# The last 256 output features of a two-layer trunk computed token-major in two halves of the tokens, each half finished and written on its own

## The chip, the cores and the metric

The kernel runs on one core of a Trainium2 chip. The metric is the device time of one execution in microseconds, as the median of several runs. A difference of 0.3% is 6.5 us here.

## The reference

Two pre-norm residual layers act on 256 tokens of 2048 features, all in float32. Each layer is a mixer followed by an MLP, and the output is a last RMSNorm of the residual stream. Only the end of the second layer and that norm matter here:

```python
def rms_norm(x, g):
    xf = x.astype(jnp.float32)
    y = xf * lax.rsqrt(jnp.mean(xf * xf, axis=-1, keepdims=True) + NORM_EPS)
    return (y * g.astype(jnp.float32)).astype(x.dtype)

def squared_relu_mlp(h, w_up, w_down):
    return jnp.square(jax.nn.relu(h @ w_up)) @ w_down
...
        h = rms_norm(x, mlp_norm[layer])
        x = x + squared_relu_mlp(h, w_up[layer], w_down[layer]).astype(x.dtype)
    return rms_norm(x, final_norm)
```

The last norm needs, for each token, the sum of squares over all 2048 features. So no feature of a token can be written before its last feature is known.

## The kernel before

The residual stream is kept feature-major in eight tiles `xT[0]` to `xT[7]`, each of 128 partitions x 2 x 256 tokens, so that a tile holds 256 features of all 256 tokens. Every weight chunk of 128 x 1024 floats is split into a rounded part `hi` (ScalarE, line 1336) and the rest `lo` (VectorE, line 1347). The activations are split the same way, and a product takes hi x hi, hi x lo and lo x hi, which are summed in PSUM. The work is written out in one list, `stream`, of pairs of a block and the number of one of its chunks. Line 1445 walks over it. A small scheduler, `jobs`, counts ticks, one per chunk here, and starts side jobs when they are due. On each engine, instructions run in the order in which the program issues them.

In the last MLP the hidden features are in eight groups. Six of them go through products that are summed in DRAM (`sums`), and come back token-major as `hs["sum", cb]`. The last two groups are multiplied at the end: eight blocks of 256 output features, `b` = 0 to 7, each with four chunks of four 128-row pieces of the weights (`eights`, line 1177). Blocks 0 to 6 are of kind "T": the weights are the stationary side and the 256 tokens (hi and lo side by side, 512 columns) the moving one. Ahead of a block's last chunk `add_sums` (line 1147) adds the transposed `hs["sum"]` to `xT[b]`. When a block ends, `down_done` (line 1162) adds the result to `xT[b]` and `final_block` (line 1228) starts a job, due two ticks later. The job adds the squares to `acc` (line 246 to 247), transposes the tile to token-major (line 1243) and stores it, times the gain, into the output tile `o` of 128 x 2 x 2048 (line 1245).

Block 7 is of kind "last". It has two PSUM regions in one tile, `ps[0]` and `ps[1]`, one in each of two PSUM banks, for its two groups of 128 features. Its last chunk does all of `ps[0]` ahead of all of `ps[1]` (line 449). Then `last_block` (line 1249) scales by `rB`, adds to `xT[7]`, squares, sums over partitions by matmuls with a column of ones (line 1262), transposes (line 1266), raises the mean to the power -0.5 on GpSimd (line 1278) and scales the whole output tile in four column quarters. VectorE takes the first 128 tokens (line 1284) and ScalarE the others (line 1285). SyncE issues eight writes of 256 KB (line 1287).

Functions that stay but are called by the change: `temp` and `side` give rotating buffers, three in SBUF and two in PSUM, and `banks(name, 1)` gives a PSUM tile of two banks.

Of the kernel before, what the change touches and what calls it, by code (L numbers as in the profile page):

```python
# [10 lines left out]
F32 = mybir.dt.float32  # L11
F32R = mybir.dt.float32r
BF16 = mybir.dt.bfloat16
AF = mybir.ActivationFunctionType
OP = mybir.AluOpType
X = mybir.AxisListType.X

P = 128
T = 256
D = 2048  # L20
KT = D // P
FF = 8192
EPS = 1e-6
# [22 lines left out]
class Jobs:  # L46
# [21 lines left out]
    def need(self, key):  # L68
        rounds = 0
        while key not in self.done:  # L70
            last = self.owner[key]
            for job in list(self.jobs):
                if job in self.jobs and not job[3]:
                    self.step(job)
                if key in self.done or job is last and rounds < 8:
                    break
            rounds += 1
# [49 lines left out]
class Block:  # L127


    def __init__(self, kind, chunks, mov, done, tiles=2, take=None, extra=None):  # L130
        self.extra = extra
        self.kind, self.chunks, self.mov, self.done, self.tiles = kind, chunks, mov, done, tiles
        self.total = len(chunks) if kind == "S" else sum(len(c.kts) for c in chunks)
        self.take = take
        self.count, self.ps = 0, None


# [1 line left out]
def trunk(ctx, tc, x, attn_norm, mlp_norm, w_up, w_down, ev_w_in, ev_q_norm, ev_w_uq, ev_kv_norm,  # L139
          ev_w_ukv, ev_w_out, od_w_in, od_sinks, od_w_out, final_norm, c_perm, c_rope, c_dist, out):  # L140
    nc = tc.nc
# [6 lines left out]
    jobs = Jobs(2)  # L148
# [10 lines left out]
    def side():  # L159
        return psum.tile([P, 512], F32, name="side", bufs=2)  # L160

    def temp():
        return tmp.tile([P, 2, T], F32, name="t", bufs=3)
# [36 lines left out]
    def banks(name="mm", bufs=3):  # L200

        return st["banks"].tile([P, 2, 512], F32, name=name, bufs=bufs)
# [232 lines left out]
    def add(block):  # L435
        for i in range(len(block.chunks)):
            stream.append((block, i))

    def consume(block, i, hi, lo):
        if block.kind == "S":  # L440
            return consume_products(block, i, hi, lo)
        if block.ps is None:
            block.ps = (block.take or banks)()
        ps, tiles, kts = block.ps, block.tiles, block.chunks[i].kts
        hi = hi[:, 0:len(kts) * tiles * P].rearrange("p (k c) -> p k c", c=tiles * P)
        lo = lo[:, 0:len(kts) * tiles * P].rearrange("p (k c) -> p k c", c=tiles * P)
        if block.kind == "N":
            order = [(n, tok) for n in range(len(kts)) for tok in range(2)]
        elif block.kind == "last" and block.count + len(kts) == block.total:
            order = [(n, j) for j in range(tiles) for n in range(len(kts))]  # L450
        else:
            order = [(n, j) for n in range(len(kts)) for j in range(tiles)]
        if block.extra and block.count + len(kts) == block.total:
            block.extra(ps)
        for n, j in order:
            m = block.mov(kts[n])
            first, last = block.count + n == 0, block.count + n == block.total - 1
            if block.kind == "N":
                o = ps[:, j, 0:T]
                xh, xl = m[:, j * P:(j + 1) * P], m[:, T + j * P:T + (j + 1) * P]  # L460
                mm(o, xh, hi[:, n], start=first, stop=False)  # L461
                mm(o, xh, lo[:, n], start=False, stop=False)  # L462
                mm(o, xl, hi[:, n], start=False, stop=last)  # L463
                continue
            c = slice(j * P, (j + 1) * P)
            if block.kind == "last":
                mm(ps[j], hi[:, n, c], m[:, 0:T], start=first, stop=False)
                mm(ps[j], hi[:, n, c], m[:, T:], start=False, stop=False)
                mm(ps[j], lo[:, n, c], m[:, 0:T], start=False, stop=last)
            else:  # L470
                if not last:
                    mm(ps[:, j], hi[:, n, c], m, start=first, stop=False)  # L472
                mm(ps[:, j, 0:T], lo[:, n, c], m[:, 0:T], start=False, stop=False)  # L473
                if last:
                    mm(ps[:, j], hi[:, n, c], m, start=False, stop=True)  # L475
        block.count += len(kts)
        if block.count == block.total:
            block.done(ps)

    def consume_products(block, i, hi, lo):  # L480

# [481 lines left out]
    def mlp(layer, last):  # L963
# [29 lines left out]
        def take_free(b):  # L993
            return lambda: banks(f"s{b % 2}", 1)

        def take_last():
            ps = banks("s1", 1)
            return [ps[:, j, 0:T] for j in range(2)]

        def up_done(grp, b):  # L1000
            def f(ps):
                t = temp()
# [144 lines left out]
        def add_sums(b):  # L1147

            def f(ps):
                need(("sum", b // 2))  # L1150
                need(("rB", n0))
                g, turned, t = hs["sum", b // 2], side(), temp()
                for j in range(2):
                    for tok in range(2):
                        nc.tensor.transpose(turned[:, j * T + tok * P:j * T + (tok + 1) * P],
                                            g[:, tok, b % 2, j * P:(j + 1) * P], ident)
                rB = E.setdefault("rB", st["rB"])
                tt(t, turned.rearrange("p (j t) -> p j t", t=T), rB[:, None, :].to_broadcast([P, 2, T]), op=OP.mult)
                tt(xT[b], xT[b], t, op=OP.add)
            return f  # L1160
# [58 lines left out]
        for b in range(8):  # L1219
            w = eights(wd, b * T, (NGRP - NS) * W // P)  # L1220
            if last and b == 7:
                add(Block("last", w, h_mov, lambda ps: last_block(E, ps), take=take_last, extra=add_sums(b)))
            else:
                add(Block("T", w, h_mov, down_done(b), take=take_free(b), extra=add_sums(b)))
        return open_pool, pool_ctx.close
# [2 lines left out]
    def final_block(E, b):  # L1228
        if b == 0:
            new_phase()  # L1230
            st["o"] = res.tile([P, 2, D], F32, name="xs")

        def job():
            yield 2, 1
            squares(b)
            if b == 6:
                acc = st["acc"]
                tt(acc[:, 0], acc[:, 0], acc[:, 1], op=OP.add)
            ps = side()
            pv = ps.rearrange("p (t c) -> p t c", c=T)  # L1240
            for tok in range(2):
                for j in range(2):
                    nc.tensor.transpose(pv[:, tok, j * P:(j + 1) * P], xT[b][:, j, tok * P:(tok + 1) * P], ident)
            fn = E["fn"](b * T, T)
            tt(st["o"][:, :, b * T:(b + 1) * T], pv, fn[:, None, :].to_broadcast([P, 2, T]), op=OP.mult)
        jobs.spawn(job())
        jobs.step(jobs.jobs[-1])

    def last_block(E, ps):

        jobs.drain()
        o, acc, xl = st["o"], st["acc"], xT[7]
        t, sq = temp(), temp()
        for j in range(2):
            tt(t[:, j], ps[j], E["rB"], op=OP.mult)
            tt(xl[:, j], xl[:, j], t[:, j], op=OP.add)
            act(sq[:, j], xl[:, j], AF.Square)
        sums, turn = banks("up", 1), side()

        def add_up(a, first, last):  # L1260
            for tok in range(2):
                mm(sums[:, tok, 0:1], a[:, tok * P:(tok + 1) * P], ones[:, 0:1], start=first, stop=last)

        def turn_out(j):
            for tok in range(2):
                nc.tensor.transpose(turn[:, j * T + tok * P:j * T + (tok + 1) * P], xl[:, j, tok * P:(tok + 1) * P], ident)
            c0 = 7 * T + j * P
            tt(o[:, :, c0:c0 + P], turn[:, j * T:(j + 1) * T].rearrange("p (t c) -> p t c", c=P),
               E["fn"](c0, P)[:, None].to_broadcast([P, 2, P]), op=OP.mult)

        add_up(acc[:, 0], True, False)
        turn_out(0)
        add_up(sq[:, 0], False, False)
        add_up(sq[:, 1], False, True)
        ms = tmp.tile([P, 2], F32, name="ms", bufs=2)
        nc.vector.tensor_scalar(ms, sums[:, :, 0], 1.0 / D, EPS, op0=OP.mult, op1=OP.add)
        r = res.tile([P, 2], F32, name="r", bufs=2)
        nc.gpsimd.tensor_tensor(r, ms, mhalf, op=OP.pow)
        turn_out(1)
        ov = out.rearrange("b (t p) d -> p (b t) d", p=P)  # L1280
        W = D // 4
        for q in range(4):
            c = slice(q * W, (q + 1) * W)
            nc.vector.tensor_scalar(o[:, 0, c], o[:, 0, c], r[:, 0:1], None, op0=OP.mult)
            act(o[:, 1, c], o[:, 1, c], AF.Copy, scale=r[:, 1:2])
            for tok in range(2):
                nc.sync.dma_start(ov[:, tok, c], o[:, tok, c])


    phases = []  # L1290
# [212 lines left out]
```

## Time and profile before

| what | us |
|---|---|
| median of 3 runs | 2158.56 (2158.47 to 2163.91) |
| the profiled execution's own time | 2162.11 |
| its span, first to last instruction | 2160.3 |
| last matmul of block 7 starts | 2147.44 |
| first write of the output is issued | 2152.16 |

Times in the rows are microseconds from the start of the span. PE is TensorE, PEld its weight load, DVE VectorE, ACT ScalarE, POOL GpSimd, SP SyncE; a q behind a name is the engine's instruction queue. "L1262" is line 1262 of the kernel.

### The profile page before, as it was taken

What the parts mean: (1) busy time and instruction counts of PE and PEld (TensorE: products, weight loads), DVE (VectorE), ACT (ScalarE), POOL (GpSimd) and SP (SyncE); (2) the same over time, 40 slices, a digit from 0 to 9 for tenths busy, and PEclk for the clock granted to TensorE, in tenths of its full rate; (3) what the DMA queues carried; (4) which work ended last, traced back from release to release, by engine and by line L of the source; (5) the groups of instructions that cost most, each with busy time, mean ns of one, the idle gap of its engine ahead of it and who ended that gap; (6) DMA issues with size and microseconds to landing.
All of it is one profiled execution on the core that took longest, in us unless ns stands there. A gap on an engine that the chain in (4) does not pass through costs nothing.

```text
span 2160.3 us, 35009 instructions
## 1 busy us (share of the span) xinstructions
PE 2141.6 (99%) x14038; PEld 1949.6 (90%) x14038; DVE 1588.6 (74%) x2120; ACT 1290.0 (60%) x1777; POOL 163.1 (8%) x217
## 2 busy tenths in 40 slices
PE   9999999999999999999999999999999999999998
PEld 7898988999999999988888889989999999999887
DVE  6766666788888888857766665577888888887475
ACT  6554545676666666655545436456676767676542
POOL 0000000000000000331000000000000000013310
PEclk9999999999999999999999999999999999999999
DMA  8545446668988989997554455666788889899972
GB/s 259 179 145 163 157 167 208 204 222 247 251 239 241 249 240 258 248 283 218 174 171 142 156 176 165 161 201 195 232 245 248 241 243 244 245 252 249 291 213 87
DMA packets 313812, 459.43 MB, mean 213 GB/s; under 512 B 11865, under 2 KB 198305, under 8 KB 313649
## 3 DMA queue, kind: packets, MB, share of 16 engines
q1 hardware_dynamic: 288416, 392.32, 57.5%
q0 software_dynamic: 25200, 64.86, 15.7%
q8 instruction: 110, 1.80, 0.3%
q14 instruction: 54, 0.43, 0.1%
q10 hardware_dynamic: 32, 0.01, 0.0%
HBM read 404.73 MB, written 60.82 MB: 215 GB/s over the span
## 4 chain that ended last, share of the span: by engine, by line
PE 49%; issue 39%; DMA 8%; POOL 4%; ACT 0%; POOLq 0%; SPq 0%; DVE 0%; ACTq 0%
PE mm L472 15%; PE mm L473 8%; PE s L472 6%; DMA sums<-sums 6%; PE s L473 4%; POOL sums L1127 3%; PE mm L461 2%; PE mm L463 2%; PE mm L462 2%; PE up L472 1%; DMA sums<-stage 1%; PE mm L475 1%; PE side L352 1%; PE up L473 1%; PE s L495 1%
## 5 line engine op out<-in xcount | busy, mean ns | idle before, releaser
L1347 DVE TENSOR_TENSOR lo<-raw,hi 128x1024 fp32r<-128x1024 f32 (+2 forms) x804 | 853.7, 1082 | 210.9 <-PE mm L473 74.8
L1336 ACT ACTIVATE hi<-raw 128x1024 fp32r<-128x1024 f32 (+2 forms) x804 | 740.8, 942 | 384.1 <-PE mm L472 105.7
L472 PE MATMUL up<-xs,hi 128*128 128x512 f32 x1440 | 516.6, 396 | 0.0
L473 PE MATMUL up<-xs,lo 128*128 128x256 f32 x1536 | 423.5, 281 | 0.0
L472 PEld LDWEIGHTS up<-xs,hi 128*128 128x128 f32 x1440 | 270.6, 188 | 57.2
L472 PE MATMUL mm<-xs,hi 128*128 128x512 f32 x885 | 319.6, 401 | 0.8 <-ACT hi L1336 0.8
L473 PEld LDWEIGHTS up<-xs,lo 128*128 128x128 f32 x1536 | 289.1, 188 | 2.2
L494 PE MATMUL s<-lo,hs 128*128 128x256 f32 x1008 | 282.9, 281 | 0.0
L493 PE MATMUL s<-hi,hs 128*128 128x256 f32 x1008 | 282.9, 281 | 0.0
L495 PE MATMUL s<-hi,hs 128*128 128x256 f32 x1008 | 282.7, 280 | 0.0
L473 PE MATMUL mm<-xs,lo 128*128 128x256 f32 x944 | 259.1, 280 | 0.2 <-DVE lo L1347 0.2
L1347 DVE TENSOR_TENSOR lo<-w,hi 128x1024 fp32r<-128x1024 f32 x144 | 175.7, 1220 | 56.7 <-ACT hi L1336 56.7
L472 PEld LDWEIGHTS mm<-xs,hi 128*128 128x128 f32 x885 | 166.0, 188 | 38.4 <-ACT hi L1336 1.3
L493 PEld LDWEIGHTS s<-hi,hs 128*128 128x128 f32 x1008 | 189.9, 188 | 6.5
L494 PEld LDWEIGHTS s<-lo,hs 128*128 128x128 f32 x1008 | 189.7, 188 | 2.1
L495 PEld LDWEIGHTS s<-hi,hs 128*128 128x128 f32 x1008 | 190.0, 189 | 0.0
L1336 ACT ACTIVATE hi<-w 128x1024 fp32r<-128x1024 f32 x144 | 151.8, 1054 | 60.4 <-DVE w L1074 56.9
L473 PEld LDWEIGHTS mm<-xs,lo 128*128 128x128 f32 x944 | 177.3, 188 | 3.2 <-DVE lo L1347 0.7
L472 PE MATMUL s<-xs,hi 128*128 128x512 f32 x480 | 171.1, 397 | 5.4 <-ACT stage L1122 3.8
L473 PE MATMUL s<-xs,lo 128*128 128x256 f32 x512 | 141.1, 281 | 0.0
L1122 ACT ACTIVATE stage<-s 128x1024 f32<-128x1024 f32 x96 | 98.2, 1023 | 71.4 <-PE s L495 57.5
L472 PE MATMUL s<-hs,hi 128*128 128x512 f32 x360 | 129.9, 399 | 0.0
(330 smaller groups left out, 3702.3 us busy)
## 6 DMA issues: line engine op xcount, KB each, us to landing
raw<-w_up SPq DMA_DIRECT2D x128, 1024.0 KB, 5.6
raw<-w_down SPq DMA_DIRECT2D x128, 1024.0 KB, 5.7
sums<-stage POOLq DMA_DIRECT2D x96, 512.0 KB, 8.5
raw<-od_w_in SPq DMA_DIRECT2D x36, 1024.0 KB, 5.0
raw<-ev_w_in SPq DMA_DIRECT2D x30, 1024.0 KB, 5.4
raw<-ev_w_out SPq DMA_DIRECT2D x16, 1024.0 KB, 5.0
raw<-od_w_in SPq DMA_DIRECT2D x20, 512.0 KB, 4.2
sums<-sums POOLq DMA_DIRECT2D x64, 128.0 KB, 6.7
```

What stands on the lines that cost most here:

```text
L461: mm(o, xh, hi[:, n], start=first, stop=False)
L462: mm(o, xh, lo[:, n], start=False, stop=False)
L463: mm(o, xl, hi[:, n], start=False, stop=last)
L472: mm(ps[:, j], hi[:, n, c], m, start=first, stop=False)
L473: mm(ps[:, j, 0:T], lo[:, n, c], m[:, 0:T], start=False, stop=False)
L493: mm(ps, x[:, a, 0:P], hi[:, w], start=(i, o) == bank[0], stop=False)
L494: mm(ps, x[:, a, 0:P], lo[:, w], start=False, stop=False)
L495: mm(ps, x[:, a, P:], hi[:, w], start=False, stop=(i, o) == bank[-1])
L1122: act(stage, ps.rearrange("p b c -> p (b c)"), AF.Copy)
L1127: nc.gpsimd.dma_start(to, stage, accum_op=OP.add)
L1336: act(d, r, AF.Copy)
L1347: tt(d, r, f32(h), op=OP.subtract)
```

## The change

Block 7 becomes kind "tail". The activations are now the stationary side (128 tokens at a time) and 256 columns of the weights the moving one, so its result is token-major: `ps[:, tok, 0:256]` for the two halves `tok` of the tokens, in the two banks of one PSUM tile. Chunks arrive as before. For each the first half's 12 matmuls run at once, and the chunk is held. At the fourth chunk the order is: remaining jobs, `begin`, the first half's last 12 matmuls, the second half's 12 for chunk 0, `middle`, the second half's other 36, `end`.

`begin` transposes `xT[7]` (four transposes) and makes `base`, which is the token-major sum `g` times `r` plus the turned `xT[7]`; it stands in for `add_sums` of block 7. `middle` sums `acc`, the squares of blocks 0 to 6, over partitions into `rest` and finishes the first half. `finish` reads the PSUM half, takes the squares of the 256 features with ScalarE's accumulator, raises the mean to the power -0.5, scales that half's row of `o` in four pieces and issues four writes, two on SyncE's queue and two on ScalarE's. The job of block 6 is due three ticks later in place of two.

```diff
@@ consume @@
-        elif block.kind == "last" and block.count + len(kts) == block.total:
-            order = [(n, j) for j in range(tiles) for n in range(len(kts))]
...
+        if block.kind == "tail":
+            return consume_tail(block, kts, hi, lo)
...
+    def consume_tail(block, kts, hi, lo):
+
+        block.held.append((kts, hi, lo))
+        begin, middle, end = block.done
+
+        def half(tok, held):
+            for kts, hi, lo in held:
+                for n, kt in enumerate(kts):
+                    m, o = block.mov(kt), block.ps[:, tok, 0:T]
+                    xh, xl = m[:, tok * P:(tok + 1) * P], m[:, T + tok * P:T + (tok + 1) * P]
+                    mm(o, xh, hi[:, n], start=kt == 0, stop=False)
+                    mm(o, xh, lo[:, n], start=False, stop=False)
+                    mm(o, xl, hi[:, n], start=False, stop=kt == block.total - 1)
+        block.count += len(kts)
+        if block.count == block.total:
+            jobs.drain()
+            begin()
+        half(0, block.held[-1:])
+        if block.count == block.total:
+            half(1, block.held[:1])
+            middle(block.ps)
+            half(1, block.held[1:])
+            end(block.ps)
@@ mlp @@
-                add(Block("last", w, h_mov, lambda ps: last_block(E, ps), take=take_last, extra=add_sums(b)))
+                add(Block("tail", w, h_mov, last_block(E, lambda: (need(("sum", 3)), hs["sum", 3][:, :, 1])[1]),
+                          take=take_free(b)))
@@ final_block @@
-            yield 2, 1
+            yield 2 + (b == 6), 1
@@ last_block (the old body, quoted by its lines above, is removed whole) @@
+        def begin():
+
+            turned, g, r = side(), sums(), st["r"]
+            base = L["base"] = temp()
+            for tok in range(2):
+                for j in range(2):
+                    nc.tensor.transpose(turned[:, tok * T + j * P:tok * T + (j + 1) * P],
+                                        xT[7][:, j, tok * P:(tok + 1) * P], ident)
+            for tok in range(2):
+                stt(base[:, tok], g[:, tok], r[:, tok:tok + 1], turned[:, tok * T:(tok + 1) * T],
+                    op0=OP.mult, op1=OP.add)
+
+        def finish(tok, ps):
+            o, t, ms = st["o"], L["t"], L["ms"]
+            one = slice(tok, tok + 1)
+            x7 = t[:, tok]
+            stt(x7, ps[:, tok, 0:T], st["r"][:, one], L["base"][:, tok], op0=OP.mult, op1=OP.add)
+            act(L["sq"][:, tok], x7, AF.Square, accum_out=L["own"][:, one])
+            stt(ms[:, one], L["own"][:, one], 1.0 / D, L["rest"][:, one], op0=OP.mult, op1=OP.add)
+            r = L["r"][:, one]
+            nc.gpsimd.tensor_tensor(r, ms[:, one], mhalf[:, one], op=OP.pow)
+            for c in (slice(0, 512), slice(512, 1024)):
+                nc.vector.tensor_scalar(o[:, tok, c], o[:, tok, c], r, None, op0=OP.mult)
+                nc.sync.dma_start(ov[:, tok, c], o[:, tok, c])
+            stt(o[:, tok, c7:], x7, r, E["fn"](c7, T), op0=OP.mult, op1=OP.mult)
+            for c, whole in ((slice(1024, 1408), slice(1024, 1408)), (slice(1408, c7), slice(1408, D))):
+                act(o[:, tok, c], o[:, tok, c], AF.Copy, scale=r)
+                nc.scalar.dma_start(ov[:, tok, whole], o[:, tok, whole])
+
+        def middle(ps):
...
+            part = banks("up", 1)
             for tok in range(2):
+                mm(part[:, tok, 0:1], st["acc"][:, 0, tok * P:(tok + 1) * P], ones[:, 0:1], start=True, stop=True)
+            nc.vector.tensor_scalar(L["rest"], part[:, :, 0], 1.0 / D, EPS, op0=OP.mult, op1=OP.add)
+            finish(0, ps)
+
+        return begin, middle, lambda ps: finish(1, ps)
```

## Rows read from the trace of the kernel before

**Rows 1.** The page: span, and busy time of each engine.

```profile
span 2160.3 us, 35009 instructions
...
PE 2141.6 (99%) x14038; PEld 1949.6 (90%) x14038; DVE 1588.6 (74%) x2120; ACT 1290.0 (60%) x1777; POOL 163.1 (8%) x217
```

**Rows 2.** Windows of the end: length, busy us (instructions), granted clock, DMA share, GB/s.

```profile
2145.00:2150.00 5.00, 4.13 (x34) 3.76 (x32) 3.21 (x7) 0.83 (x2) 0.00 (x0) 1.00 0.00 0
2150.00:2155.00 5.00, 0.82 (x6) 0.58 (x6) 2.26 (x6) 2.56 (x4) 0.71 (x1) 0.61 0.41 152
```

**Rows 3.** Timeline, TensorE in block 7: start, length, what [idle before <-releaser].

```profile
2135.18 0.28 PE L467 MATMUL s<-hs,hi 128*128 128x256 f32 x1
...
2140.94 0.60 PE L1243 MATMUL side<-misc,xT 128*128 128x128 f32 x4
2141.29 0.36 PE L467 MATMUL s<-hs,hi 128*128 128x256 f32 x1
...
2146.00 0.28 PE L469 MATMUL s<-hp,lo 128*128 128x256 f32 x1
...
2147.44 0.28 PE L469 MATMUL s<-hp,lo 128*128 128x256 f32 x1
2147.56 0.50 PE L1262 MATMUL up<-ones,acc 128*128 128x1 f32 x4
2148.79 0.41 PE L1266 MATMUL side<-misc,xT 128*128 128x128 f32 x2 [0.73 <-DVE xT L1256]
```

**Rows 4.** Timeline, the other engines in and behind block 7.

```profile
2138.07 1.22 DVE L1347 TENSOR_TENSOR lo<-raw,hi 128x1024 fp32r<-128x1024 f32 x1
...
2139.92 0.42 DVE L1238 TENSOR_TENSOR acc<-acc 128x256 f32<-128x256 f32 x1
...
2147.76 0.42 DVE L1255 TENSOR_TENSOR t<-s,rB 128x256 f32<-128x256 f32 x1 [1.46 <-PE s L469]
2148.22 0.42 DVE L1256 TENSOR_TENSOR xT<-xT,t 128x256 f32<-128x256 f32 x1
...
2148.74 0.42 ACT L1257 ACTIVATE t<-xT 128x256 f32<-128x256 f32 x1 [9.86 <-DVE xT L1256]
...
2150.65 0.16 DVE L1276 TENSOR_SCALAR ms<-up 128x2 f32<-128x2 f32 x1 [0.88 <-PE up L1262]
...
2150.90 0.71 POOL L1278 TENSOR_TENSOR r<-ms,mhalf 128x2 f32<-128x2 f32 x1 [75.36 <-DVE ms L1276]
2151.64 2.56 ACT L1285 ACTIVATE xs<-xs,r 128x512 f32<-128x512 f32 x4 [1.76 <-POOL r L1278]
2151.65 1.68 DVE L1284 TENSOR_SCALAR xs<-xs,r 128x512 f32<-128x512 f32 x4 [0.36 <-POOL r L1278]
2152.16 4.48 SPq L1287 DMA_DIRECT2D out<-xs  x8
```

**Rows 5.** DMA, 2140.0 to 2160.3: 40 slices of 0.51 us; writes' landing.

```profile
GB/s 0 0 0 0 0 0 32 0 0 0 0 0 0 0 0 0 0 0 0 0 0 0 0 0 0 121 383 379 375 379 391 383 379 383 387 383 186 0 0 0
...
out<-xs SPq DMA_DIRECT2D x8, 256.0 KB, 2.9
```

**Rows 6.** Timeline, TensorE with activations stationary and weights moving, in the products.

```profile
1980.55 0.28 PE L493 MATMUL s<-hi,hs 128*128 128x256 f32 x1
...
1982.56 0.28 PE L495 MATMUL s<-hi,hs 128*128 128x256 f32 x1
```

**Rows 7.** Timeline, ScalarE at the start, and Square with its accumulator read.

```profile
0.74 0.46 ACTq L178 DMA_DIRECT2D t<-attn_norm  x1
1.23 1.28 ACT L1379 ACT_TABLE_LOAD   x1 [1.23 <-PEq L1489]
...
43.42 0.40 ACT L1394 ACTIVATE t<-oT 128x256 f32<-128x256 f32 x1
43.73 0.19 ACT L1394 ACTIVATION_READ_ACCUMULATOR t<-oT 128x1 f32 x1
```

**Rows 8.** One line of the code: GpSimd's slowest powers.

```profile
L565 POOL TENSOR_TENSOR lr<-ms,mhalf x2: 1068/1902/2737, 77.4 to 91.6; 128x2 f32<-128x2 f32 x2
```

More of the change, by code (lines that the diff above doesn't have):

```diff
@@ L133, in __init__ @@
         self.total = len(chunks) if kind == "S" else sum(len(c.kts) for c in chunks)
-        self.take = take
+        self.take, self.held = take, []
         self.count, self.ps = 0, None
@@ L465, in consume @@
             c = slice(j * P, (j + 1) * P)
[L466 to L475, printed above, removed]
+            if not last:
+                mm(ps[:, j], hi[:, n, c], m, start=first, stop=False)
+            mm(ps[:, j, 0:T], lo[:, n, c], m[:, 0:T], start=False, stop=False)
+            if last:
+                mm(ps[:, j], hi[:, n, c], m, start=False, stop=True)
         block.count += len(kts)
@@ L994, in take_free @@
             return lambda: banks(f"s{b % 2}", 1)
-        def take_last():
-            ps = banks("s1", 1)
-            return [ps[:, j, 0:T] for j in range(2)]
         def up_done(grp, b):
@@ L1247, in final_block, with last_block @@
         jobs.step(jobs.jobs[-1])
[L1249 to L1260, printed above, removed]
+    def last_block(E, sums):
+        ov = out.rearrange("b (t p) d -> p (b t) d", p=P)
+        c7 = 7 * T
+        L = {}
+        def begin():
+            turned, g, r = side(), sums(), st["r"]
+            base = L["base"] = temp()
@@ L1261, in add_up @@
             for tok in range(2):
-                mm(sums[:, tok, 0:1], a[:, tok * P:(tok + 1) * P], ones[:, 0:1], start=first, stop=last)
-        def turn_out(j):
+                for j in range(2):
+                    nc.tensor.transpose(turned[:, tok * T + j * P:tok * T + (j + 1) * P],
+                                        xT[7][:, j, tok * P:(tok + 1) * P], ident)
             for tok in range(2):
[L1266 to L1285, printed above, removed]
+                stt(base[:, tok], g[:, tok], r[:, tok:tok + 1], turned[:, tok * T:(tok + 1) * T],
+                    op0=OP.mult, op1=OP.add)
@@ L1286, in last_block @@
+        def middle(ps):
+            L["t"], L["sq"] = temp(), temp()
+            for name in ("ms", "own", "rest"):
+                L[name] = tmp.tile([P, 2], F32, name="l" + name)
+            L["r"] = res.tile([P, 2], F32, name="r", bufs=2)
+            part = banks("up", 1)
             for tok in range(2):
-                nc.sync.dma_start(ov[:, tok, c], o[:, tok, c])
+                mm(part[:, tok, 0:1], st["acc"][:, 0, tok * P:(tok + 1) * P], ones[:, 0:1], start=True, stop=True)
+            nc.vector.tensor_scalar(L["rest"], part[:, :, 0], 1.0 / D, EPS, op0=OP.mult, op1=OP.add)
+            finish(0, ps)
```

## Prediction

> **What bounds the kernel now.** The page comes first: TensorE is busy in 99% of a span of 2160.3 us [rows 1], so up to the last matmul only its work counts. The change touches none of that up to block 7, so I read the end of the span alone. The windows show where TensorE stops: 4.13 us of work from 2145 to 2150, then 0.82 us in the next five [rows 2]. The timeline of TensorE gives the block. It starts at 2135.18, and 48 matmuls bring it to 2140.94, so one takes 0.12 us of the queue [rows 3]. Its last matmul starts at 2147.44 [rows 3]. From there to the end are 12.9 us without weights to multiply: a stretch of latencies, and then one of bandwidth.
>
> The latencies are in the timeline of the other engines. VectorE sees the PSUM result at 2147.76; adds, squares, column sums and a power follow, and the scaling starts at 2151.64. The first write is issued at 2152.16 [rows 4]. So last matmul to scaling is 4.20 us, and scaling to first issue 0.52 us. The bandwidth is in the DMA view: data flow without a gap from inside slice 25 (from 2152.7) to the middle of slice 36 (about 2158.5), at 375 to 391 GB/s [rows 5]. Eight writes of 256 KB are 2.10 MB. At 382 GB/s they take 5.5 us, and the DMA engines are the limit there, not the issues.
>
> **The matmuls of block 7.** 96 of 128 x 128 x 256 stay 96 of that size with the sides exchanged. The products already run that way: 17 steps from 1980.55 to 1982.56, 0.118 us each [rows 6]. This costs nothing. The four transposes ahead of the last chunk stay as well, with another tile: four such take 0.35 us (2140.94 to 2141.29), as before [rows 3]. The job of block 6 moves from behind 48 matmuls to behind 36, and its four transposes with it; no wait arises, since its `xT[6]` is ready when VectorE starts the `lo` split at 2138.07 [rows 4], and 36 matmuls end at 2139.50. That `lo` split, of the last chunk, ends at 2139.29 [rows 4], ahead of the last chunk's start near 2140.2.
>
> **Added on TensorE.** The sums of `acc` stood behind the block (four passes, 0.50 us with the last one's tail [rows 3]) and now stand in it, ahead of 36 matmuls: about 0.45 us of queue. `acc` is ready at 2140.34 [rows 4], so they needn't wait. Counting 60 matmuls at 0.12, two sets of transposes and these sums from 2135.18, TensorE would be through with them at 2143.5. The same count for the old block gives 2147.28 where the row has 2147.44 [rows 3], so I use 2143.7.
>
> **The disputed wait.** The first half's `finish` reads bank 0 of a PSUM tile while 36 matmuls into bank 1 of it are still to come. The old block has a similar place. `ps[0]`, in its own bank, was complete with the matmul at 2146.00 [rows 3], and VectorE had nothing to do, yet its first read sat idle for 1.46 us and began at 2147.76, behind the last matmul into `ps[1]` [rows 3, 4]. So the program treats both banks of a tile as one thing. If it does so here, TensorE's next matmul waits until VectorE has read: the tail and signal of the sums 0.15 us, `rest` and the step to the next instruction 0.2 us, the read 0.42 to 0.48 us, and 0.15 us back (2148.64 to 2148.79 [rows 3, 4]): 0.9 us. If it doesn't, it costs 0. No row shows a matmul that waits for a read of another bank. The nearest row is that of the read that did wait, so I take 0.9 and keep 0 for the range.
>
> The Trainium skill, page "PSUM — Partial Sum Buffer", section "PSUM bank collisions raise a hardware error", says that PSUM is to be guarded by bank and quadrant, and its summary that a read beside running matmuls should target a different bank, which this one does. By that rule the wait needn't exist, and the sum would be 0.9 us lower; the row above speaks the other way for this program, whatever the chip would allow.
>
> **The chain behind the last matmul.** It now starts at 2147.44 + 0.45 + 0.9 = 2148.79. From rows: 0.32 us until VectorE reads (2147.44 to 2147.76), 0.52 until ScalarE starts on the result (2148.22 to 2148.74) [rows 4], 0.49 for Square and the read of its accumulator (43.42 to 43.92) [rows 7] and 0.06 of signal, 0.25 from a small VectorE instruction to GpSimd and 0.74 from there to the scaling (2150.65, 2150.90, 2151.64) [rows 4]. That is 2.38 in place of 4.20: no adds to `xT[7]`, no eight passes of column sums, no transposes behind the block. The saving is 1.82 us. The scaling starts at 2151.17, 0.47 us ahead of before. GpSimd's power is the unsafe term: 0.71 us in its row here [rows 4], up to 2.74 elsewhere [rows 8]. Nothing else is on GpSimd at the end [rows 2], as at the row with 0.71, so I take that; the other end is +2.0 us.
>
> **The writes.** For the first half, VectorE reads at about 2144.05, and the same chain brings its scaling to 2146.1. SyncE issues at 2146.6 and 2147.0. ScalarE copies 384 columns (between 0.42 us for 256 and 0.71 for 512 [rows 4]: 0.56), issues (0.46 [rows 7]), copies and issues again, and is free at 2148.15. The square of the second half needs it at 2149.63. VectorE is free at 2147.3 and needed at 2149.1. The data, 1.05 MB, need 2.75 us and pass from 2147.5 to 2150.3, 2 us ahead of the second half's first packet. So the first half is wholly covered by the second's matmuls. If that cover were gone, it would cost those 2.75 us again.
>
> For the second half, issue and first packet stand as far behind the scaling as before (0.52 us and 0.85 more). The last issue, the second on ScalarE's queue, comes near 2152.8 and its 0.33 MB alone would end near 2154.5, but all 1.05 MB at 382 GB/s end at 2155.3, so bandwidth still sets the end. The data take 2.75 us less than before. What follows the last byte stays.
>
> **The sum.** -0.47 - 2.75 = -3.2 us. The span becomes 2157.1, the profiled execution 2158.9 in place of 2162.11. The median of the runs shown is 3.6 us under that execution; the change applies to both alike: 2158.56 - 3.2 = 2155.3 us.
>
> **The rivals.**
> 1. No wait between the banks. For it: it needs only a finer bookkeeping than the row of the read shows. Against it: that row. 0.9 us more gain: 2154.4 us. This is also the outcome by the rule of the Trainium skill's PSUM page above.
> 2. ScalarE is held by its own writes (the other side: slower). The square of the second half stands behind two issues on ScalarE's queue. If an issue held the engine for H, the square would be late by 2H - 2.4 us, and the second half's last write by H - 1.2 more. At 2.9 us, the time to landing of the old writes [rows 5], that is 5.1 us against the gain of 3.2: 2160.5 us, slower than before; it decides from H = 2.3 us on. Against it: at the start ScalarE issued a DMA at 0.74 and began its next instruction at 1.23 [rows 7]. For it: by the code that DMA moves only 16 rows of 512 bytes, and no row shows ScalarE issuing a large one.
> 3. The clock. TensorE pauses 0.9 us in mid-block; were the granted clock to fall from 2.4 to 1.2 GHz behind that, the last 36 matmuls would take 4.3 us more: 2159.6 us, which is 1 us slower than before. For it: the clock falls to a mean of 0.61 in the window from 2150, where TensorE is busy 0.82 us [rows 2]. Against it: a pause of 0.73 us lies ahead of 2148.79 [rows 3], and the window around it still has 1.00 [rows 2].
> 4. The change doesn't shorten the chain, because the power is slow (2.74 us): +2.0 us, 2157.4 us. For it: the rows of line 565 [rows 8]. Against it: 0.71 in the same place [rows 4].
>
> **How the numbers follow.** Forecast 0.55, rival 1 0.25, rival 2 0.06, rival 3 0.06, rival 4 0.08. A measurement can tell some 0.3% of this kernel, 6.5 us, from no change. No case leaves that band (2152.1 to 2165.0): the whole gain is 3 to 4 us of 2159. So "same" holds nearly all: 0.94, and 0.03 on either side for what no row shows. The range: its low end is rival 1 with the sums on TensorE hidden after all (-0.45): 2153.9, and 0.6 below that, a quarter of the 2.38 us of the chain, whose terms come from single rows: 2153.3. Its high end is the forecast with the distance between the median and the slowest run of before, 5.4 us: 2160.7, which takes in rivals 2 to 4.
>
> **What would show it.** A pause of about 0.9 us on TensorE between the sums of `acc` and the last 36 matmuls, ended by VectorE's read (in rival 1, none); 0.12 us per matmul; the old 375 to 391 GB/s in two stretches of 2.75 us, the first ended before the second power; last matmul to scaling 2.4 us; ScalarE's next instruction 0.5 us behind its first issue; a power of 0.7 us on GpSimd twice. The prediction is wrong if the first half's writes are still under way when the second's start, if ScalarE reaches the second square late, or if TensorE's matmuls behind the pause stand 0.24 us apart.

## The result and the profile after

| | before | after |
|---|---|---|
| median, 6 runs each, us | 2159.36 (2158.47 to 2166.05) | 2149.95 (2148.42 to 2152.53) |
| ratio, 95% interval | | 0.9947 (0.9936 to 0.9958) |
| profiled execution, us | 2162.11 | 2149.86 |
| its span, us | 2160.3 | 2148.1 |
| block 7's first matmul | 2135.18 [rows 3] | 2126.83 |
| from there to the end | 25.12 | 21.27 |

The change gains 0.53%, about 9.4 us. The forecast was 2155.3 us, its range began at 2153.3, and "faster" had 0.03. The last two lines say where to look. Of the 12.2 us between the two spans, 3.85 lie behind block 7's first matmul, where the change is. The other 8.35 lie ahead of it, where its code does nothing. These are two single executions, and that of before was 2.75 us above its median; by the medians 9.4 - 3.85, some 5.6 us, lie ahead of block 7.

First the part that was forecast. TensorE's timeline of the changed kernel, from block 7's first matmul (the rows before: [rows 3]):

```profile
2126.83 0.28 PE L485 MATMUL s<-hi,hs 128*128 128x256 f32 x1
...
2134.78 0.50 PE L1307 MATMUL up<-ones,acc 128*128 128x1 f32 x4
2135.92 0.38 PE L485 MATMUL s<-hi,hs 128*128 128x256 f32 x1 [0.64 <-DVE t L1287]
...
2140.00 0.28 PE L487 MATMUL s<-hi,hp 128*128 128x256 f32 x1
```

The pause is there: 0.64 us on TensorE behind the sums, and VectorE's read ends it. The timeline of the other engines of the changed kernel from there on (before: [rows 4]):

```profile
2135.32 0.16 DVE L1308 TENSOR_SCALAR lrest<-up 128x2 f32<-128x2 f32 x1 [1.94 <-PE up L1307]
2135.39 0.47 DVE L1287 SCALAR_TENSOR_TENSOR t<-s,r,t 128x256 f32<-128x256 f32 x1
...
2136.82 0.57 POOL L1291 TENSOR_TENSOR r<-lms,mhalf 128x1 f32<-128x1 f32 x1 [70.33 <-DVE lms L1289]
...
2138.07 0.36 ACTq L1298 DMA_DIRECT2D out<-xs  x1
...
2138.48 0.62 ACT L1297 ACTIVATE xs<-xs,r 128x384 f32<-128x384 f32 x1 [0.44 <-ACT xs L1297]
2139.13 0.34 ACTq L1298 DMA_DIRECT2D out<-xs  x1
2140.31 0.48 DVE L1287 SCALAR_TENSOR_TENSOR t<-s,r,t 128x256 f32<-128x256 f32 x1 [1.61 <-PE s L487]
2140.83 0.42 ACT L1288 ACTIVATE t<-t 128x256 f32<-128x256 f32 x1 [1.73 <-DVE t L1287]
...
2141.37 0.16 DVE L1289 SCALAR_TENSOR_TENSOR lms<-lown,lrest 128x1 f32<-128x1 f32 x1 [0.57 <-ACT t L1288]
2141.62 0.55 POOL L1291 TENSOR_TENSOR r<-lms,mhalf 128x1 f32<-128x1 f32 x1 [4.23 <-DVE lms L1289]
...
2142.20 0.88 DVE L1293 TENSOR_SCALAR xs<-xs,r 128x512 f32<-128x512 f32 x2 [0.67 <-POOL r L1291]
```

From the last matmul (2140.00) to the scaling (2142.20) it is now 2.20 us. ScalarE goes on 0.41 us behind the start of an issue, and its second square waits for VectorE, not for the DMAs. The DMA view of 2127.8 to 2148.1, in slices of 0.51 us (before: [rows 5]):

```profile
GB/s 0 0 0 0 0 0 0 0 0 0 0 0 32 0 0 0 0 0 0 0 0 109 379 379 379 391 399 30 0 0 0 359 366 385 387 388 182 0 0 0
...
out<-xs SPq DMA_DIRECT2D x4, 256.0 KB, 2.5
out<-xs ACTq DMA_DIRECT2D x2, 320.0 KB, 3.0
out<-xs ACTq DMA_DIRECT2D x2, 192.0 KB, 2.6
```

The output leaves in two stretches at the old rate, and the first has ended before the second begins.

Now the part that was not forecast. A window of equal length in the first MLP, in which TensorE is busy throughout at full clock, shows it. The columns are those of [rows 2]; first the kernel before:

```profile
500.00:700.00 200.00, 200.00 (x1404) 186.50 (x1403) 167.96 (x216) 137.59 (x167) 15.59 (x18) 1.00 0.90 242
```

The changed kernel:

```profile
500.00:700.00 200.00, 200.00 (x1419) 186.12 (x1418) 170.04 (x218) 138.47 (x169) 15.55 (x18) 1.00 0.90 245
```

Same clock, no idle time, 15 more matmuls in 200 us. Which kind became quicker is seen in the timeline of the changed kernel, at two runs of 17 steps through products (before: [rows 6], 0.118 us a step):

```profile
599.29 0.28 PE L512 MATMUL s<-hi,hs 128*128 128x256 f32 x1
...
601.29 0.28 PE L514 MATMUL s<-hi,hs 128*128 128x256 f32 x1
...
604.21 0.28 PE L512 MATMUL s<-hi,hs 128*128 128x256 f32 x1
...
606.14 0.28 PE L514 MATMUL s<-hi,hs 128*128 128x256 f32 x1
```

The first run steps by 0.1176 us as before, the second by 0.1135. There are 4,176 such products. Over all of them the starts are 116.2 ns apart, before 118.0: 4,176 x 1.8 ns is 7.5 of the 8.35 us. Waits differ between the traces as well. Near 2004 us TensorE of the kernel before waits for a ScalarE copy; the like wait of the changed kernel, at 1997.11, is 0.71 us long:

```profile
2004.36 0.80 PE L472 MATMUL s<-xs,hi 128*128 128x512 f32 x1 [2.09 <-ACT stage L1122]
```

The diff touches no product, but it does change an address. `middle` takes three tiles of 128 x 2 floats from the pool `tmp`, which lies ahead of the pools of the four phases. In the compiled program each takes 32 bytes per partition, so every tile of the phases stands 96 bytes higher. (The addresses here and below are those of the compiled programs; the traces do not hold them.) The `h` tiles, stationary in the products, go from 224 to 320 modulo 512 bytes; the split weights `hi` and `lo`, moving there, stay at 128.

### The profile page after: what moved, and what is told of

The parts are those of the page before. It is cut to its first block, busy times and chain, and to the rows that moved or that the text cites. A ratio compares the mean times of both kernels' runs of the same rounds, so it can differ in the third digit from the quotient of the medians.

```text
span 2148.1 us, 34987 instructions
## 1 busy us (share of the span) xinstructions
PE 2132.4 (99%) x14026; PEld 1939.9 (90%) x14026; DVE 1586.2 (74%) x2120; ACT 1289.3 (60%) x1779; POOL 163.1 (8%) x218
## 4 chain that ended last, share of the span: by engine, by line
PE 56%; issue 35%; DMA 5%; POOL 3%; ACT 0%; DVE 0%; POOLq 0%; SPq 0%; ACTq 0%
PE mm L467 15%; PE s L467 10%; PE mm L468 8%; PE s L468 5%; DMA sums<-sums 3%; POOL sums L1142 3%; DMA sums<-stage 2%; PE mm L463 2%; PE mm L462 2%; PE mm L461 2%; PE up L467 1%; PE mm L470 1%; PE side L352 1%; PE up L468 1%; PE s L513 1%
```

## The experiments

The theory (**place**): the place of the phases' tiles sets the products' pace, and the rewritten block gives only 3 to 4 us. The rivals: the block gives it all and the pace is chance (**tail**), any move would do, or other tiles than `h` matter. Beside each ratio stands its 95% interval; "products" is the mean distance of the starts of two products that follow each other.

**1 and 2: the move without the change.** Two lines are added to the kernel before; run 2 has 16 in place of 24 floats.

```diff
     def last_block(E, ps):
...
+        pad = tmp.tile([P, 24], F32, name="pad")
+        nc.gpsimd.memset(pad, 0.0)
         t, sq = temp(), temp()
```

> The kernel before with 96 unused bytes per partition set once by GpSimd ahead of the last block, in the pool where the change keeps its three small tiles; nothing of the change itself. Every tile of the four phases then starts where it starts in the changed kernel, at 0 and no longer at 32 modulo 64 bytes. If the place of the tiles is what shortened the matmuls (place theory): 5.5 to 8.4 us less than before, about 2151 to 2154 us, the products' matmuls 113 to 116 ns apart in the first MLP instead of 118. If all of the gain comes from the rewritten last block (tail theory): the time of before, 2159 us, and 118 ns.

> The same with 64 unused bytes: the tiles move, but stay at 32 modulo 64 bytes. If the place modulo 64 bytes counts: the time of before, 2159 us, the products' matmuls 118 ns apart. If any move, or the extra instruction, does it: 2151 to 2154 us like the 96 bytes. Tail theory: 2159 us.

Measured: 96 bytes 0.9962 (0.9948 to 0.9976), 2152.84 against 2161.65 us, products 115.3 ns. 64 bytes 1.0025 (1.0012 to 1.0037), 2166.34 us, products 119.5 ns. The window of the kernel with 96 bytes:

```profile
500.00:700.00 200.00, 200.00 (x1417) 186.11 (x1416) 170.07 (x218) 138.54 (x168) 15.59 (x18) 1.00 0.89 244
```

The same window of the kernel with 64 bytes:

```profile
500.00:700.00 200.00, 200.00 (x1389) 186.03 (x1389) 166.32 (x213) 137.49 (x167) 15.59 (x18) 1.00 0.88 240
```

And 17 of its steps in the timeline, 0.1194 us each:

```profile
606.88 0.28 PE L493 MATMUL s<-hi,hs 128*128 128x256 f32 x1
...
608.91 0.28 PE L495 MATMUL s<-hi,hs 128*128 128x256 f32 x1
```

So 96 unused bytes, with nothing of the change, give 8.8 us: the tail theory falls. But 64 bytes were to change nothing, and they cost 4.7 us. Place counts, though not as I had it, modulo 64.

**3: the change without the move.**

```diff
-                L[name] = tmp.tile([P, 2], F32, name="l" + name)
+                L[name] = E["pool"].tile([P, 2], F32, name="l" + name)
```

> The changed kernel with its three small tiles put at the end of the last phase's own pool, so that every other tile starts where it starts in the kernel before; all of the rewritten last block is kept. Place theory: only what the last block itself gives is left, 3.2 to 3.9 us less than before, about 2155.5 us, products' matmuls 118 ns apart. Tail theory: like the changed kernel, 2150 us.

Measured: 0.9990 (0.9980 to 1.0001), 2158.42 us, 3.2 us below before; products 118.0 ns; from block 7's first matmul (2131.65) to the end 21.35 us. Its window:

```profile
500.00:700.00 200.00, 200.00 (x1402) 186.42 (x1402) 167.95 (x216) 137.45 (x167) 15.58 (x18) 1.00 0.89 242
```

This is what the forecast spoke of, and it is near what it said: -3.2 us. The interval just reaches no change. This trace, too, has block 7 start 3.53 us earlier than the trace of before, with the products at the old pace: so much can lie between two executions without any change of place. Runs 1 and 3 together, 0.38% and 0.10%, make nearly the whole of the change's 0.53%, and within the intervals all of it.

**4: only the `h` tiles.** Each `h` tile of the kernel before becomes 64 bytes wider, and its contents begin 32 bytes in.

```diff
-  h = E["pool"].tile([P, 7, 2 * P], F32R, name="hs", ...)
+  h = E["pool"].tile([P, 14 * P + 16], F32R, name="hs", ...)
+  h = h[:, 8:8 + 14 * P].rearrange("p (o t) -> p o t", t=2 * P)
```

> The kernel before with only the h tiles (the hidden layer in its high and low halves, stationary in the products and moving elsewhere) starting at 0 modulo 64 bytes; all other tiles of the phases stay at 32. If the weight loads of h set the products' pace: 5.5 to 8.4 us less than before, 2151 to 2154 us, and 113 to 116 ns between products in the first MLP. If the gain is in other tiles (the raw weights' split, the products' moving operand, the elementwise work): 2159 us and 118 ns.

Measured: 0.9994 (0.9984 to 1.0003), 2159.60 us, the time that was expected if other tiles count; but the products are 117.2 ns apart, as neither case had it. As each tile was 64 bytes wider, the eight tiles stood at eight places modulo 512. Matching every product of the trace with the addresses in the compiled program:

```
h tile, modulo 512      0    64   128   192   256   320   384   448
products, ns        118.0 118.1 119.1 113.5 118.2 114.6 119.6 116.7
```

Within one kernel, with the weights at one place, each `h` tile has its own pace: the `h` tiles alone do it, and the mean of fast and slow places is what hid it. 320 is where the change had put all of them.

**5 to 7: three places foretold from that table.** Runs 5 and 6 are run 1 with 120 and 40 floats; run 7 is the changed kernel with such a tile of 96 floats.

> The kernel before with 480 unused bytes: the h tiles start at 192 modulo 512 bytes. In the run that moved only the h tiles, tiles at 192 modulo 512 gave products 113.5 ns apart. If the pace goes by the place modulo 512: 4.5 ns less for each of 4,176 products, some 19 us less than before, about 2142 us. If it goes by the place modulo 64 alone (192 is 0 modulo 64, as with the 96 bytes): 115.3 ns and some 8 us less, about 2153 us.

> The same with 160 unused bytes: the h tiles start at 384 modulo 512 bytes, which is 0 modulo 64 too. Place modulo 512: 119.6 ns, as tiles at 384 had in the run that moved only the h tiles, some 6 us more than before, about 2167 us. Place modulo 64: 115.3 ns, some 8 us less, about 2153 us.

> The changed kernel with 384 unused bytes more, so that its h tiles go from 320 to 192 modulo 512 bytes. If place and tail add up: 113.5 ns between products and about 11 us less than the changed kernel, some 2139 us, the best of all. Place modulo 64: no change from the changed kernel, 2150 us.

Measured: run 5 0.9934 (0.9917 to 0.9951), 2147.57 us, products 114.1 ns. Run 6 1.0038 (1.0025 to 1.0050), 2170.84 us, 119.3 ns. Run 7 0.9906 (0.9891 to 0.9921), 2142.13 us, 114.1 ns; before took 2161.88 us beside them. The 17 steps in run 5:

```profile
597.25 0.28 PE L493 MATMUL s<-hi,hs 128*128 128x256 f32 x1
...
599.19 0.28 PE L495 MATMUL s<-hi,hs 128*128 128x256 f32 x1
```

The step is 0.114 us. All three signs are as the table has them, and modulo 64 is out. Run 5's gain, 14.3 us, is nearly 5 us smaller than expected: the products came to 114.1 and not 113.5 ns, which is 2.5 us, and of the 16.3 us that they save 14.3 reach the end. Run 7 lies 19.8 us below before, where the expected 2139 us are 20.4 below the 2159.36 of the first comparison. Run 6's loss, 9.0 us, is 3 us larger; its products explain 5.4 of it.

**8: a PSUM tile for each half.**

```diff
+        def take_two():
+            a, b = banks("s1", 1), banks("s0", 1)
+            return [a[:, 0], b[:, 0]]
...
-                    m, o = block.mov(kt), block.ps[:, tok, 0:T]
+                    m, o = block.mov(kt), block.ps[tok][:, 0:T]
```

> The changed kernel with a PSUM tile of its own for each half of the tokens in the last block, so that the second half's matmuls never share a tile with what the first half's VectorE operation reads. If TensorE's pause of 0.64 us ahead of the second half's second chunk is the wait on that tile: the pause is gone from the timeline and the stretch from block 7's first matmul to the end is 0.6 us shorter (20.6 instead of 21.3 us). If something else holds TensorE there (the sums, the weights): the pause stays.

Measured: 0.9936 (0.9921 to 0.9951), 2148.48 us; 20.61 us from block 7's first matmul (2128.59) to the end. TensorE's timeline at the place of the pause, and VectorE's read of the first half:

```profile
2136.54 0.50 PE L1311 MATMUL up<-ones,acc 128*128 128x1 f32 x4
2136.91 0.37 PE L485 MATMUL s<-hi,hs 128*128 128x256 f32 x1
...
2137.16 0.47 DVE L1291 SCALAR_TENSOR_TENSOR t<-s,r,t 128x256 f32<-128x256 f32 x1
...
2137.58 0.28 PE L487 MATMUL s<-hi,hs 128*128 128x256 f32 x1
```

The pause is gone, and the stretch is 0.66 us shorter. VectorE reads its half while the matmuls run on, so the wait came from the shared tile, in the program, and not from the chip. That agrees with the rule weighed in the prediction, of the Trainium skill's page "PSUM — Partial Sum Buffer", section "PSUM bank collisions raise a hardware error".

**9 and 10: the place of one operand, or the distance of the two?** Both are the changed kernel with 64 bytes ahead of the weights, so `hi` and `lo` stand at 192; a tile of 80 (run 9) or 96 floats (run 10) in `tmp` then puts `h` at 192 or 256.

```diff
+    ahead = wts.tile([P, 16], F32, name="ahead")
+    nc.gpsimd.memset(ahead, 0.0)
     NG = 72
```

> The changed kernel with 64 unused bytes ahead of the weights' tiles, and 320 in the last pool: the split weights go from 128 to 192 modulo 512 bytes, xs from 480 to 32, the h tiles from 320 to 192. In the products the moving operand then stands at 192 as well as the stationary one; in the blocks with xs the stationary weights stand at 192. If the place of the stationary operand alone sets the pace: products 114.1 ns apart, and the 256-column matmuls with xs 113 to 115 ns in place of 118; with 2,992 of these at 256 and as many at 512 columns some 12 to 25 us below the kernel with the h tiles at 192 alone (2142 us), so about 2117 to 2130 us. If the distance from the moving operand sets it (192 - 128 = 64 was good, 0 was 119.1): products about 119 ns, matmuls with xs unchanged at about 118 (their distance of 160 stays), about 2163 us.

> As the run before, but 384 bytes in the last pool: h tiles at 256 modulo 512 bytes, 64 above the moving weights at 192 as in the fast kernels. Place of the stationary operand alone: products 118.2 ns as tiles at 256 had in the run that moved only the h tiles, so some 17 us above its neighbour of this set. Distance: 114.1 ns, some 20 us below its neighbour.

Measured: run 9 1.0025 (1.0015 to 1.0034), 2165.44 us, products 119.3 ns. Run 10 0.9916 (0.9899 to 0.9934), 2143.13 us, 114.1 ns; before 2159.91 us. The window of run 9:

```profile
500.00:700.00 200.00, 200.00 (x1392) 186.46 (x1392) 166.47 (x214) 137.57 (x167) 15.55 (x18) 1.00 0.88 238
```

The window of run 10:

```profile
500.00:700.00 200.00, 200.00 (x1426) 185.96 (x1425) 170.38 (x218) 138.71 (x167) 15.54 (x18) 1.00 0.90 247
```

`h` at 192 was the best place and is now a bad one; 256, in run 4's table at 118.2 ns no better than before, is now good. So it is the stationary tile's distance from the moving one, modulo 512, that counts, and not its own place: 64 is fast, 0 slow.

**11: the first half's write, not hidden.** Every operation stays, but the first half's DMAs are queued behind the second's.

```diff
-                nc.sync.dma_start(ov[:, tok, c], o[:, tok, c])
+                for w in [1, 0][:2 * tok]:
+                    nc.sync.dma_start(ov[:, w, c], o[:, w, c])
```

(The writes on ScalarE's queue alike.)

> The changed kernel with every operation kept, but each DMA of the first half's output queued behind the second half's on the same queue, so that none of the first half is written beside the matmuls. If the write hidden beside the matmuls is the larger part of what the last block gives: 2.75 us more from block 7's first matmul to the end (24.0 instead of 21.3), about 2152.7 us. If the shorter chain alone did it: the stretch stays near 21.3 us.

Measured: 0.9963 (0.9951 to 0.9976), 2152.10 us; 24.16 us from block 7's first matmul (2122.54) to the end. The DMA view of run 11, from 2126 to 2146.7:

```profile
GB/s 0 0 0 0 0 0 0 32 0 0 0 0 0 0 0 0 0 0 0 0 0 0 0 0 0 4 380 354 378 376 368 368 403 369 405 381 267 0 0 0
```

One stretch again, of twice the length, and 2.89 us more: the hidden write is worth what the forecast gave it.

**12: both together**, run 8 with run 7's tile.

> The changed kernel with the two PSUM tiles and with the h tiles at 192 modulo 512 bytes. If both gains add: 0.6 us below the kernel with the h tiles at 192 alone, about 2141.5 us, with products 114.1 ns apart and 20.6 to 20.8 us from block 7's first matmul to the end.

Measured: 0.9912 (0.9892 to 0.9931), 2141.60 us; products 114.1 ns, end stretch 20.42 us. The stretch is 0.2 us shorter than the 20.6 to 20.8 expected; the time is no longer told from run 7's, whose interval overlaps.

**13 and 14: other matmuls, other distances.** Run 13 is run 12 with `gT` 24 floats wider and the tile in `tmp` at 72 floats; run 14 is run 4 with the contents at the tile's first byte.

> The best kernel so far with gT 96 bytes wider, so that xs goes from 480 to 64 modulo 512 bytes and the weights, stationary there at 128, stand 64 above it, as the h tiles at 192 stand 64 above the moving weights in the products. If the distance sets the pace of every matmul: the 256-column matmuls with xs 114 ns apart instead of 118 and those of 512 columns 229 instead of 233, some 12 to 24 us less than the best so far (2141.6 us), so 2118 to 2130 us. If it is particular to the products: the matmuls with xs stay at 118 and 233 ns, 2141.6 us.

> The kernel before with the h tiles 64 bytes wider each and started at their first byte, so that the eight tiles stand at 32, 96, 160, 224, 288, 352, 416 and 480 modulo 512 bytes, the moving weights at 128. If the distance sets the pace: tiles at 224 give 118.0 ns and tiles at 288 give 119.5, as the kernels with all tiles there, whatever the neighbours; the other six are not known. If the order of the tiles or the neighbour in time counts: other values for these two.

Measured: run 13 0.9906 (0.9885 to 0.9927), 2141.26 us. Products 113.8 ns; the matmuls that move `xs` stay at 118.2 and 233.9 ns (118.0 and 233.3 in run 12). Run 14 0.9991 (0.9979 to 1.0002), 2160.57 us:

```
h tile, modulo 512     32    96   160   224   288   352   416   480
products, ns        119.5 116.8 118.6 119.0 118.8 117.5 118.3 118.5
```

Both fall against the simple rule. The distance that serves the products does nothing for the matmuls that move `xs`. Others do follow a place: where the `h` tiles are the moving side, in the last blocks of each layer, a matmul of 512 columns takes from start to start 230.5 ns in run 5 and 231.0 in run 10 (distance 64), but 234.2 in run 6 (256) and 235.2 in run 9 (0). And a tile at 224 gives 119.0 where the kernel before has 118.0, one at 288 gives 118.8 where run 2 has 119.5. So the distance modulo 512 tells fast from slow, but not the last nanosecond.

## Why the prediction was wrong

**The step that failed** is in its first paragraph: "The change touches none of that up to block 7, so I read the end of the span alone." No instruction there was touched, but the operands' addresses were. That step put at nothing what was 8.35 us between the two traces and some 5.6 us by the medians. Runs 1 and 3 show it from both sides (the move alone 8.8 us, the new block alone 3.2), and the outcome "same" at 0.94 rested on it: from the end of the span alone no case could leave the band of 0.3%.

**What was read from the end of the span held**, with two terms a little off in size:

| from block 7's first matmul | forecast | measured |
|---|---|---|
| last matmul later | +1.35 | +0.91 (13.17 for 12.26) |
| of this, the disputed wait | 0.9 | 0.64 |
| last matmul to scaling | -1.82 | -2.00 (2.20 for 4.20) |
| scaling to the end | -2.75 | -2.76 (5.90 for 8.66) |
| sum | -3.2 | -3.85 |

The wait is a chain of four: sums to `rest` 0.04, `rest` to the read 0.07, the read 0.47, back to TensorE 0.06. I had 0.15, 0.2, 0.42 to 0.48, and 0.15: the read was right, the three steps around it too long. The other 0.18 of the first line is mostly the products' pace: the 32 steps from 2136.37 to 2140.00 take 0.113 us each, 0.005 less than [rows 6]. GpSimd's power took 0.55 where 0.71 was used, which is most of the 0.18 in the chain.

**The rivals.** 1, no wait: the wait was there, 0.64 us; run 8 shows that it need not be. 2, ScalarE held by its writes: an issue took 0.34 to 0.36 us, far from the 2.3 at which it would decide. 3, the clock: the steps behind the pause are the 0.113 us above, not 0.24. 4, a slow power: 0.57 and 0.55 us.

**What stays open** is why the distance counts. While one product streams its moving operand, the next one's stationary operand is loaded (in run 1's window 186.11 us of loads stand in 200 us that are all matmul); a clash of these two reads would fit runs 9 and 10, but no run shows the reads themselves, and run 13 shows matmuls that this distance does not help. The Trainium skill, page "TensorE: Matmul & The Clock Gate", section "Step-by-step: what each phase is for", has the two reads go through two ports, so that loading the next weights takes no read bandwidth of SBUF from the running matmul; the step of 113.5 to 119.6 ns by place alone is hard to join with that, and the measurement stands. Open too is what happens at a distance of 192, in the changed kernel and runs 1, 8 and 11. There the products have two paces and none between: the mean of each of the 336 chunks of products is either 113.3 to 113.8 or 117.6 to 118.0 ns, like the two runs of steps shown for the changed kernel. The quicker pace has 115 chunks in the changed kernel, 123 in run 8, 191 in run 1 and 189 in run 11; the 115.3 to 116.2 ns are means over both. Run 11 differs from the changed kernel only in the order of its last DMAs, so something beside the distance picks the pace, and no run shows what.

## What to carry to other kernels

A new tile moves every tile that is allocated behind it, and here 96 bytes were worth more than the edit they came with. Before a gain is put down to an edit, compare the tiles' addresses of the two programs, or allocate the new tiles behind everything (run 3). In the traces, lay the same matmuls side by side from the start: a difference that grows along the span is a pace, one that comes at a place is a wait; where TensorE is the bound, counting matmuls in windows of equal length tells it in one row.

Half of a write is hidden if its rows are finished while the other half still multiplies, and that was worth the data's own time (2.75 us forecast, 2.89 in run 11). Halves that are read and written at different times want a PSUM tile each.

## What the runs showed of the hardware

The step between two 128 x 128 x 256 matmuls of this kernel's products, at an unchanged clock of 1.00, lies between 113.5 and 119.6 ns by where the stationary tile starts relative to the moving one. With all `h` tiles at one place the distances modulo 512 gave: 64, 113.8 to 114.1 ns (runs 5, 7, 10, 12, 13); 192, 115.3 to 116.2 as a mean of 113.5 and 117.8; 96, 118.0; 0 and 256, 119.3; 160, 119.5. Over 4,176 products, 114.1 and 119.3 ns are 22 us apart; runs 5 and 6, whose code differs only in 120 against 40 unused floats, are 23 us apart (2147.57 and 2170.84), 1.1% of the time.
